# Nested self-attention on one core: loop bodies of two to four tiles written as lists with named PSUM banks, V tiles scaled on ScalarE, and pairs that fall from 512 to 448 and from 160 to 128 rows

## The chip, the cores and the metric

The kernel runs on one core of a Trainium2 chip. The metric is the device time of one execution in microseconds; lower is better. Engines are named as in the profile: PE (matrix engine; PEld is its weight load), DVE (VectorE), ACT (ScalarE), POOL (GpSimd) and SP (SyncE, which here only issues DMAs).

## The reference

```
batch, max_seq, n_heads, head_dim = (32, 512, 8, 64)
lengths = np.random.randint(64, max_seq, size=batch)        # the same draw each time
x: [32, 512, 512] float32, w_qkv: [512, 1536] float32
for b in range(batch):
    x_b = x[b, :lengths[b]]
    q, k, v = split(x_b @ w_qkv)              # 8 heads of 64
    attn = softmax(q @ k.T / 8)               # per head
    output[b, :lengths[b]] = attn @ v         # the other rows are zero
```

## The kernel before

The kernel sorts the 32 sequences by length, longest first, and takes them in pairs. A pair has a class: the row count, out of 512, 480, ... 96 and 340, that holds its longer sequence. For each class there is a loop body, built ahead of time, and all engines branch from body to body by a table of the classes. A body has two **halves**. A half does the attention of one sequence (N rows) and, between its steps, the projections (Q, K, V) of the next one (W rows), so that PE has matmuls while ACT takes exponentials. T is the number of 128-row tiles of N. With the lengths drawn here the halves run in this order (N to W):

| pair | lengths | halves before |
|---|---|---|
| 1 | 502, 447 | 512 to 512, 512 to 480 |
| 2 | 446, 436 | 448 to 448, 448 to 416 |
| 3 | 363, 357 | 384 to 384, 384 to 352 |
| 4, 5 | 351, 347; 343, 333 | 352 to 352 twice; 352 to 340, 340 to 340 |
| 6, 7 | 323, 315; 310, 261 | 340 to 320, 320 to 320; 320 to 288, 288 to 288 |
| 8 | 260, 257 | 288 to 288, 288 to 256 |
| 9, 10 | 246, 230; 223, 220 | 256 to 256, 256 to 224; 224 to 224 twice |
| 11, 12 | 216, 183; 164, 152 | 224 to 192, 192 to 192; 192 to 160, 160 to 160 |
| 13, 14 | 143, 140; 134, 119 | 160 to 160 twice; 160 to 160, 160 to 128 |
| 15, 16 | 101, 86; 79, 75 | one tile: 128 to 96, 96 to 96; 96 to 96, the last |

A pair *drops* when its second sequence is one class lower: the body `drops[N]` then lays the second half at the lower row count. Before the change this is so only inside one tile count and up to 384 rows. Three-tile halves up to 340 rows are *dense*: the scores of one head pair over all key tiles fill both score banks without gaps and are exponentiated in two instructions.

The order of the work in a half is a list of tokens. `S` is a group of score matmuls and its exponential, `D` the dense form; `Q`, `K`, `B` (both) project one head pair for the next sequence; `E` and its end `F`/`G`/`H`/`I` project Q and K in two passes of 64 contraction rows each, in two banks at once; `U`/`W` does the same for two V tiles; `V` is one V tile; `A`/`Z` is the product of probabilities and V for a head pair, with `R` the reciprocal of the row sums and `X` the scaling into `onat`; `O` issues half of the output store from ACT; `c` reads the next class. Scores and `E`/`U` matmuls have 64 contraction rows (64*128 in the profile) and run two at a time; the other projections and `A` have 128. A last V tile of at most 64 rows is done by `vsides` as two column halves side by side (128*64).

PSUM has two score slots of two banks (`s0`, `s1`, tile psc) and four single banks (`a0`, `a1`, tile pa; `v0`, `v1`, tile pav). PE takes a bank with `acquire` (it waits for the engine that emptied it last) and `evacuate` hands it on: Q and K are copied by DVE or ACT (L439, L440), V tiles are always scaled by the row mask on DVE (L463, L559, L560). With `turns` (three-tile halves and 416, 448) the four banks go round; otherwise projections alternate between `a0` and `a1` and `A` takes `v0` and `v1` together.

SP works through its own list for each half: wait until PE has read `xT[h]` (semaphore `s_xtf`), issue the DMA transposes of the next sequence into it (L1603; PE waits for them in `start_proj`), wait for POOL's cast and load the sequence after that (L1614, L1618), zero fill (L1535), store the second half of the output (L1527). POOL writes the ones column of V (L1968, L1969), for which PE waits at the last V tile (`s_on`), and casts x (L1962). Where two-tile bodies end, `bridge` makes the scores for the first one-tile half; there SP stages a transpose (L1740) that POOL copies (L2012).

## Time and profile before

| | us |
|---|---|
| timed runs | 331.85, 333.05, 334.75 (median 333.05) |
| profiled execution: span of the profile | 330.1 |
| PE busy | 316.4 |
| ACT busy | 242.4 |
| DVE busy | 203.6 |
| POOL busy | 68.7 |

The page gives the profiled execution by its span, from the first to the last instruction; a timed run holds, beside such a span, what lies before and after it. Matmuls are pipelined and their ends are modelled, so that successive ones overlap in the profile: how far apart they start says more than how long each shows. In a row, a tile's name stands as output<-inputs, then the shape, then xcount; a stage of the kernel is read by giving a window in us from the span's start.

### The profile page before, as it was taken

How to read it: one execution, taken by the hardware profiler on the slowest of the kernel's cores; microseconds unless marked ns; L12 is line 12 of the kernel's file. 1: busy time of each engine (PE TensorE's matmuls, PEld its weight loads, DVE VectorE, ACT ScalarE, POOL GpSimd, SP SyncE). 2: the span in 40 equal slices, each digit the busy share in tenths (PEclk: the TensorE clock that was granted, in tenths of full speed). 3: DMA queues.
4: the chain of work that ended last, by engine and by line, in shares of the span. 5: the costliest groups of instructions: out<-in, count | busy, mean ns of one | idle time of the engine just before them, and what ended most of it. 6: DMA issues, size and time to landing. Idle time of an engine off the chain costs nothing. (4 is left out here: it accounts for less than half of the span.)

```text
span 330.1 us, 12320 instructions
## 1 busy us (share of the span) xinstructions
PE 316.4 (96%) x4353; PEld 205.5 (62%) x4354; DVE 203.6 (62%) x587; ACT 242.4 (73%) x358; POOL 68.7 (21%) x135
## 2 busy tenths in 40 slices
PE   7899999999999999999999999999999999999880
PEld 2565445455565656656666677677777777677750
DVE  3576576656585575576476557655755566767662
ACT  4577878788889879878778887787677676566531
POOL 3452220201111201210220222022111131131331
PEclk9999999999999999999999999999999999999996
DMA  6957599987656996985997999897689979965952
GB/s 195 341 138 263 94 375 310 292 179 279 153 194 142 326 263 145 323 286 149 283 314 169 235 319 216 214 291 235 212 139 174 214 199 183 170 201 148 200 145 70
DMA packets 83289, 72.42 MB, mean 219 GB/s; under 512 B 41660, under 2 KB 64188, under 8 KB 83204
## 3 DMA queue, kind: packets, MB, share of 16 engines
q1 hardware_dynamic: 69700, 58.27, 70.0%
q10 hardware_dynamic: 13504, 13.11, 11.8%
q8 instruction: 42, 0.69, 0.8%
q14 instruction: 43, 0.35, 0.4%
HBM read 25.32 MB, written 36.70 MB: 188 GB/s over the span
## 5 line engine op out<-in xcount | busy, mean ns | idle before, releaser
L367 ACT ACTIVATE ep<-psc 128x896 f16<-128x896 f32 (+9 forms) x184 | 146.8, 847 | 44.0 <-PE psc L324 34.0
L324 PE MATMUL pa<-xT,w_r 128*128 128x160 f16 (+19 forms) x952 | 127.8, 277 | 1.2 <-PEq L62 1.2
L324 PEld LDWEIGHTS pa<-xT,w_r 128*128 128x128 f16 (+1 forms) x952 | 73.0, 97 | 29.2 <-issue 10.1
L324 PE MATMUL psc<-qkT 64*128 64x224 f16 (+17 forms) x700 | 66.7, 285 | 0.6 <-ACT ep L408 0.4
L324 PE MATMUL pa<-w_r,xT 128*128 128x512 f16 (+4 forms) x332 | 58.6, 328 | 0.3 <-DVE v_aug L560 0.3
L324 PE MATMUL pav<-xT,w_r 64*128 64x352 f16 (+12 forms) x384 | 58.3, 306 | 0.0
L440 DVE CAST qkT<-pa 128x512 f16<-128x512 f32 (+9 forms) x59 | 33.4, 566 | 40.0 <-PE pa L324 36.2
L408 ACT ACTIVATE ep<-psc 128x864 f16<-128x864 f32 (+3 forms) x56 | 49.7, 946 | 10.9 <-PE psc L324 6.5
L324 PE MATMUL pav<-v_aug,ep 128*128 128x65 f16 x1268 | 54.9, 194 | 1.7 <-PEq L62 1.7
L1968 POOL MEMSET v_aug<- 128x256 f16 x28 | 8.8, 313 | 225.5 <-POOLq L1519 225.5
L324 PEld LDWEIGHTS pav<-v_aug,ep 128*128 128x128 f16 x1268 | 48.8, 98 | 10.0 <-issue 3.0
L439 ACT CAST qkT<-pa 128x320 f16<-128x320 f32 (+8 forms) x74 | 34.2, 466 | 16.6 <-PE pa L324 10.8
L661 DVE SCALAR_TENSOR_TENSOR onat<-pav,masks,rcp 128x128 f32<-128x128 f32 (+1 forms) x120 | 41.4, 384 | 4.1 <-DVE rcp L638 1.6
L1962 POOL CAST x<-x_nat 128x1536 f16<-128x1536 f32 (+3 forms) x33 | 42.0, 1272 | 8.6 <-POOLq L1519 8.3
L324 PEld LDWEIGHTS psc<-qkT 64*128 64x128 f16 x700 | 26.7, 94 | 27.2 <-issue 16.7
L463 DVE TENSOR_TENSOR v_aug<-pa,masks 128x512 f16<-128x512 f32 (+1 forms) x46 | 30.8, 674 | 15.0 <-PE pa L324 14.4
L324 PEld LDWEIGHTS pav<-xT,w_r 64*128 64x128 f16 (+1 forms) x384 | 29.8, 95 | 11.6 <-issue 1.6
L324 PEld LDWEIGHTS pa<-w_r,xT 128*128 128x128 f16 (+2 forms) x332 | 22.9, 99 | 18.3 <-issue 4.9
L324 PE MATMUL pav<-w_r,xT 128*128 128x512 f16 (+3 forms) x132 | 24.0, 333 | 0.0
L638 DVE RECIPROCAL rcp<-pav 128x8 f32<-128x8 f32 (+2 forms) x66 | 12.9, 195 | 17.5 <-PE pav L324 14.7
L324 PEld LDWEIGHTS pa<-v_aug,ep 128*128 128x128 f16 x524 | 19.3, 98 | 6.3 <-issue 2.6
L440 DVE CAST qkT<-pav 128x352 f16<-128x352 f32 (+7 forms) x27 | 14.4, 539 | 14.1 <-PE pav L324 13.4
(99 smaller groups left out, 181.4 us busy)
## 6 DMA issues: line engine op xcount, KB each, us to landing
out_dram<-zt SPq DMA_DIRECT2D x16, 768.0 KB, 5.7
x_nat<-in_x_dram SPq DMA_DIRECT2D x12, 512.0 KB
out_dram<-onat ACTq DMA_DIRECT2D x21, 256.0 KB, 3.8
x_nat<-in_x_dram SPq DMA_DIRECT2D x5, 1024.0 KB
out_dram<-onat ACTq DMA_DIRECT2D x12, 384.0 KB, 4.8
out_dram<-onat SPq DMA_DIRECT2D x12, 384.0 KB, 4.4
x_nat<-in_x_dram SPq DMA_DIRECT2D x17, 256.0 KB, 6.5
x_nat<-in_x_dram SPq DMA_DIRECT2D x4, 768.0 KB
```

The source lines that it names most:

```text
L324: return lambda e: e.matmul(o, lhsT, rhs, start=start, stop=stop)
L367: return e.activation(out=dst[at], in_=src[at], func=AF.Exp, scale=scale)
L408: lambda e, par=par, b=b: e.activation(out=ep[:, i, par, 0:T, 0:N], in_=psc_f[:, par, 0 : T * N].rearrange("p (t n) -> p t n", n=N), func= ...
L439: return lambda e: e.copy(out=dst, in_=src)
L440: return lambda e: e.tensor_copy(out=dst, in_=src)
L463: return lambda e: e.tensor_tensor(out=v_aug[h][:, t, lo // HD : lo // HD + n, 0:HD], in0=area[b][:, 0:w].rearrange("p (a d) -> p a d", d=HD),
L638: pr.add("dve", lambda e: e.reciprocal(out=rv, in_=den).then_inc(s_r, 1))
L661: ins = e.scalar_tensor_tensor(scalar=now[0][:, 1, t : t + 1], op0=ALU.mult, op1=ALU.mult, **ops)
L1962: e.tensor_copy(out=x16[h][:, 0:T, :], in_=x_nat[h][:, 0:T, :]).then_inc(s_xc[h], 1)
L1968: e.memset(v_aug[h][:, T - 1, NPAIR:NH, 0:HD], 0.0)
```

## The change

1. All half orders for two, three and four tiles are new lists in which each token names its banks and its evacuating engines: `E3ad:..` means Q by ACT, K by DVE. `e`/`E` are the two passes over Q and K, now in two-tile halves too (`two_cross`); one letter (`E1d`) empties both banks in one instruction. `A10` and `A11` are the parts of one head pair (two query tiles each with four tiles; all three with three tiles, `A10` alone); in two-tile halves `A20` takes head pairs 2 and 3 of query tile 0, and each half makes its own scores `S0` rather than those of the next sequence. `s0` and `s1` can hold a projection (`B1d:s1`).
2. `v_out` and `vsides` can scale on ACT (`V1a`): a Copy with the mask column as scale, read from a [128, 1] operand through a register.
3. Pairs of classes 512 and 480 whose second sequence fits 448 rows drop to 448, pairs of class 160 whose second sequence fits 128 rows drop to 128. Pair 1 becomes 512 to 448, 448 to 448. Pair 14 becomes 160 to 128 and then a one-tile half (`half_one`), with `fall` making its scores; the second output tile is filled with zeros and stored.
4. Second halves of `leave` follow the first halves of `stay` with different banks held (`follow`, `drain`); branch hints and alignment follow the new paths.

The lists that run with these lengths, and the core of the rest:

```diff
-        4: "S S Q0 +A0 S S K0 V0 S S Q1 +A1 S S K1 V1 S S Q2 +A2 S S K2 V2 S S Q3 +A3 S S V3 K3 O",
-        3: "k3 S S E0 E2~ S F0 S I2 S A0 A1 S U0 S S W0 E1~ S S G1 A2 Q3 O A3 S S V2",
-        2: "S S B0 b1 A0 A1 b2 S S V1 b3 A2 O A3 R3 X3 V0",
-    DENSE = "K2 q2 D E1 E3 I1 H3 D k0 c A0 Q0~ A1 D V2 O V1 A2 D A3~ V0"
-    DENSE_OUT = DENSE.replace("D A3~ V0", "V0 D A3")
-    FOUR = "S E1 S G1 S E2 S G2 S E0 S E3 S G0 G3 S S A0 Z0 V1 +A1 S S Z1 V3 +A2 S O S V0 +Z2 S A3 Z3 S S V2"
-    FOUR_SIDES = FOUR.replace("G1", "F1").replace("Z1 V3 +A2", "V3 Z1 A2")
+    LISTS = {
...
+        (512, 448): "S e2:a0,a1 S E2dd S e0:v1,v0 S E0da S e1:a0,a1 S e3:v0,v1 S E1dd S E3dd S A01:a0 A00:a1 c R00 R01 X00 X01 S A10:v0 A11:v1 S S R11 R10 X11 X10 V0d:a0 A20:v1 A21:a1 S S R21 R20 O X21 V1a:a0 X20 V2d:a1 S S V3d:v0 A30:a1 A31:v1 R30 X30 R31 X31",
...
+        448: "S e1:a0,v0 S E1dd S e3:v1,a1 S E3ad S e0:v0,a0 S e2:a1,v1 S c E0da E2dd S S V1d:v0 A00:a1 A01:a0 A10:v1 S R01 R00 X01 S X00 R10 A11:v0 R11 A20:a0 X10 V3a:a1 R20 X11 S S X20 V0d:v1 A21:a1 S A30:v0 O R21 A31:v1 X21 R30 R31 S S X30 X31 V2d:a1",
+        (448, 416): "S e3:a1,v0 S e0:a0,v1 S E3dd S E0dd S S e1:a1,v0 S e2:a0,v1 S E1da E2dd S S V3a:v0 A00:a0 A01:a1 R00 R01 X00 S X01 S c A11:v1 A10:v0 R10 R11 X10 X11 V1a:a0 S S A20:a1 A21:a0 O R20 R21 X20 X21 V0d:v1 S S A30:a1 R30 A31:a0 X30 R31 V2a:v1 X31",
...
+        384: "S e1:a1,v0 S E1d S e0:v1,a0 c S E0ad S A10:v0 A00:a1 R00 S X00 u0:a0,v1 S R10 X10 W0da S S A20:a1 K2a:v0 R20 X20 K3d:a0 S O A30:a1 R30 X30 Q3a:a0 S S Q2d:v0 V2d:a0",
+        (384, 352): "S S e0:v0,v1 e1:a1,a0 S E0ad E1da S S A00:v0 A10:v1 R00 X00 R10 S X10 u0:a1,a0 S S W0da e3:v0,v1 S S E3dd O A20:a1 R20 c X20 Q2a:a0 A30:v0 S S R30 X30 V2d:v1 K2a:a1",
+        352: "S S e0:v0,a0 e1:a1,v1 S E0ad E1da S S A10:a0 R10 A00:v0 X10 R00 S u0:a1,v1 S S X00 W0da e2:v0,a0 S S c E2da Q3a:v1 A20:a1 S S R20 A30:a0 X20 O R30 V2a:v1 X30 K3a:a1",
+        (352, 340): "S S e0:v0,a0 e3:a1,v1 S E0da E3dd S S A10:v0 A00:a1 R10 X10 S R00 u0:v1,a0 S S X00 c W0da e1:a1,v0 S S E1da A20:a0 A30:v1 R20 X20 O V2a:a1 e2:a0,v0 R30 S S X30 E2ad",
+        340: "K2d:a1 V0d:v1 D e0:v0,a1 e1:a0,v1 E0ad E1dd D Q3a:v0 A00:a0 A10:v1 Q2a:a1 R00 X00 R10 c D V1a:v0 X10 V2d:a0 K3a:v1 A20:a1 O R20 A30:a0 D X20 R30 X30",
+        (340, 320): "Q2a:v1 Q3d:v0 V1d:a1 D e0:v1,v0 V2a:a1 Q1d:a0 E0da D A00:a0 K3a:v1 R00 A10:a1 K1a:v0 X00 D R10 A20:v1 X10 R20 O K2a:v0 c X20 V0d:a1 D A30:v1 R30 X30",
+        320: "Q1a:v0 V0a:a0 D V2d:v1 K0a:a1 K1a:a0 K3a:v0 D A00:a1 Q0a:v0 R00 Q2d:v1 X00 A10:a0 R10 D A20:v0 c X10 R20 O X20 Q3d:a1 V1d:v1 D A30:a0 R30 X30 K2d:v0",
+        (320, 288): "K2a:a1 K1a:v1 D Q2d:a0 K0d:a1 Q1d:v0 Q3d:v1 D A00:a1 R00 K3d:v0 A10:v1 R10 X00 Q0a:a0 X10 D A20:v0 R20 X20 c V1a:a1 V2d:v1 D A30:v0 R30 O X30 V0a:a1",
+        288: "Q2d:a0 K3a:v1 D e0:v0,a1 e1:a0,v1 E0da c E1da D K2d:v0 Q3a:v1 A10:a0 R10 A00:a1 D X10 R00 V0a:v0 X00 A20:a0 R20 X20 V2d:v1 D O A30:a1 V1a:v0 R30 X30",
+        (288, 256): "Q2d:v1 D K3d:a1 Q0d:a0 V2d:v1 K1d:a1 D A10:v1 Q3a:a0 K0a:a1 R10 X10 A00:v0 D R00 X00 Q1d:a1 V0d:v1 A20:a0 c R20 X20 O V1d:a1 D A30:v0 R30 K2d:v1 X30",
     }
+    TWO = {
+        False: "S1 e1:a1,a0 S0 e3:v0,v1 E1da E3ad S2 S3 A00:a0 A01:v1 R00 B2a:v0 V1a:a1 X00 A20:a0 R01 X01 R20 X20 O A21:v0 R21 X21 B0a:s1 V0d:v1 c",
+        True: "S1 B1d:s1 e0:a1,a0 e3:v0,v1 E0da S0 S3 E3d c V1d:a1 S2 A00:v1 R00 X00 A01:a0 R01 B2a:s0 X01 O A21:v0 A20:a1 R2 V0a:v1 X20 X21",
+        (256, 256): "S1 S0 e1:a0,a1 E1ad e0:v1,v0 S3 E0ad S2 A00:a1 V1a:a0 A01:v0 R0 B2a:s0 A20:v1 c X01 A21:a0 R20 X00 O X20 R21 V0a:v0 X21 B3d:a1",
+        (256, 224): "S1 S0 e2:a0,v1 e0:v0,a1 c E2dd E0ad S3 S2 A01:v1 A00:a1 R00 R01 X00 X01 B1a:a0 V1d:v0 A21:a1 A20:a0 R2 O X21 X20 B3a:s1 V0d:v1",
+        (224, 192): "S1 S0 e1:a0,a1 e0:v0,v1 E1da E0dd S3 V1a:a0 S2 A00:v1 K2d:a1 Q2d:v0 B3a:s0 A01:a0 R00 X00 c R01 X01 O A20:a1 A21:v0 V0a:v1 R2 X20 X21",
+        (192, 192): "S1 B1d:s1 e0:a0,a1 e2:v1,v0 E0dd S0 E2dd S3 V1d:a0 S2 A00:v0 A01:v1 R0 X00 c X01 B3a:s0 A21:a1 A20:a0 O R2 X20 V0a:s1 X21",
+        (192, 160): "S1 B3d:a0 e1:v1,v0 S0 E1ad e0:a0,a1 S2 E0aa S3 A00:v0 V0a:v1 c R00 A01:a0 X00 R01 B2a:s0 A20:v0 A21:a1 X01 R21 O X21 R20 V1a:v1 X20",
+        (160, 128): "S1 V1d:a0 c S0 e1:v0,a1 V0a:a0 Q2d:v1 E1ad S3 S2 A00:v1 R00 K2a:v0 B0a:a0 B3a:s0 A01:a1 X00 A20:v0 R01 A21:v1 X01 O R2 X20 X21",
+    }
+    def two_order(N, W):
+        return TWO.get((N, W), TWO[W > P and half_rows(W)])
...
-    def v_out(b, h, i, T, of):
+    def v_out(b, h, i, T, of, eng="dve"):
...
+        if eng == "act":
+            def scaled(e):
+                rv = e.snap(regs_act["rank"], min_val=0, max_val=B - 1)
+                return e.activation(
+                    out=v_aug[h][:, t, lo // HD : lo // HD + n, 0:HD],
+                    in_=room[b][:, 0:w].rearrange("p (a d) -> p a d", d=HD), func=AF.Copy,
+                    scale=masks[:, bass.ds(rv, 1), 0, t : t + 1].rearrange("p o t -> p (o t)"),
+                )
...
+    def fall(pr, st, M):
+        for b in list(st["holds"]):
+            acquire(pr, b)
+        acquire(pr, "s0")
+        pr.signals.append(s_xtf[1])
+        scores(pr, 0, 1, 0, 0, 1, M)
...
+            if h and T == 2 and M <= P:
+                half_one(pr, h, W, True)
+            else:
+                half(pr, h, T, (N, M)[h], (M, W)[h], st, last and h == 1)
+            if not h and T == 2 and M <= P:
+                fall(pr, st, M)
...
-    drops = {N: make_body(N, lower[N], lower[N], turn=turn(N)) for N in CLASSES
-             if lower[N] < N and -(-lower[N] // P) == -(-N // P) and N <= 3 * P}
+    drops_at = {N: M for N, M in lower.items()
+                if M < N <= 3 * P and (-(-M // P) == -(-N // P) or M == P)}
+    drops_at.update({N: FOUR_ROWS for N in CLASSES if N > FOUR_ROWS})
+    drops = {N: make_body(N, M, M) for N, M in drops_at.items()}
```

## The prediction

> **What bounds the kernel now.** I read the page first, its head and its DMA line, then the busy time by stage (cut where the matrix engine's queue takes up a new sequence's transposed input), then the timeline of a short stretch, then two views of waits.

> ```profile
> span 330.1 us, 12320 instructions
> ...
> PE 316.4 (96%) x4353; PEld 205.5 (62%) x4354; DVE 203.6 (62%) x587; ACT 242.4 (73%) x358; POOL 68.7 (21%) x135
> ...
> DMA  6957599987656996985997999897689979965952
> ```

> PE is busy for 96% of the span. Its ends are modelled, though, so that share alone doesn't say how much a better order could win. By stage:

> ```profile
> core 0: us, PE busy (x) PEld busy (x) DVE busy (x) ACT busy (x) POOL busy (x), PEclk, DMA share, GB/s
> ...
> 24.65:62.08 37.43, 37.43 (x413) 18.80 (x414) 24.09 (x57) 29.99 (x32) 6.60 (x7) 1.00 0.92 253
> 62.08:97.13 35.05, 35.03 (x492) 20.25 (x490) 22.54 (x69) 29.40 (x38) 4.58 (x6) 1.00 0.78 232
> 97.13:157.36 60.23, 60.19 (x859) 36.51 (x856) 37.29 (x112) 50.38 (x80) 9.45 (x15) 1.00 0.79 228
> 157.36:235.61 78.25, 77.64 (x1176) 54.50 (x1173) 49.42 (x164) 61.58 (x93) 13.08 (x21) 1.00 0.93 245
> 235.61:263.36 27.75, 27.75 (x351) 20.85 (x348) 15.40 (x41) 20.55 (x28) 6.19 (x12) 1.00 0.92 193
> 263.36:311.85 48.49, 47.38 (x743) 35.90 (x741) 33.45 (x91) 31.25 (x57) 11.67 (x24) 1.00 0.84 180
> ```

> These are the 512 pair, the 448 pair, the loose three-tile halves, the dense ones, 256 and 224, and the 192 and 160 rows down to the one-tile tail. PE has work throughout at the full clock, ScalarE 64% to 84%, VectorE less. So PE ends each stage; but the DMA engines are at 0.92 and 0.93 in three of them, which matters below. What a matmul costs, and what PE loses between matmuls:

> ```profile
> 299.82 0.38 PE L324 MATMUL pa<-w_r,xT 128*128 128x512 f16 x1
> ...
> 300.13 0.45 PE L324 MATMUL psc<-qkT 64*128 64x160 f16 x8
> ...
> 300.51 1.41 PE L324 MATMUL pa<-xT,w_r 128*128 128x160 f16 x16
> ...
> 303.28 0.63 PE L324 MATMUL pa<-w_r,xT 128*64 128x256 f16 x8
> ...
> 304.99 1.04 PE L324 MATMUL pa<-w_r,xT 128*128 128x512 f16 x4
> ...
> 308.76 0.61 PE L324 MATMUL pa<-w_r,xT 128*128 128x256 f16 x4
> ```

> One 512-column matmul shows 0.38 and four show 1.04, so in a stream they start 0.22 apart. Four of 512 columns and four of 256 differ by 0.43 over 1024 columns: 0.42 ns a column. The 64-row scores run two at a time (eight of 160 columns in 0.45). Now the joints: the 512-column matmul of 299.82 lets the next start at 300.04, but the scores start at 300.13. Their four pairs take 4 x 0.07, to 300.41, but the 128-row projection starts at 300.51. So **each switch between 64-row and 128-row matmuls costs 0.09 to 0.10**, and so, I take it, does one into or out of the two-column form (128*64) of a short last V tile. What else PE's weight loads wait for inside the halves (window 24 to 311):

> ```profile
> PEld psc L324 <- ACT ep L367: 2.3, 8, 0.4
> PEld pa L324 <- DVE qkT L440: 1.6, 5, 0.4
> PEld pav L324 <- DVE qkT L440: 1.3, 4, 0.4
> ...
> PEld psc L324 <- ACT ep L408: 0.5, 1, 0.5
> PEld pa L324 <- DVE v_aug L463: 0.4, 2, 0.2
> PEld pa L324 <- DVE v_aug L560: 0.4, 1, 0.4
> ```

> 6.5 us together, in 28 halves: all that any order of evacuations can give back, and part of it lies behind a running matmul.

> **The change part by part.** The sum is made against the execution of 330.1 us span; the three timed runs are 331.85 to 334.75, so 1.8 to 4.7 lie around such a span. I take the difference off the median, 333.05.

> *512 falls to 448.* Of the drawn lengths only the first pair (502, 447) does. Its first half projects a 448-row partner: 32 Q/K matmuls and 4 pairs of scores, 64 columns fewer each, 36 x 64 x 0.42 ns = 0.97; and the last V tile goes in the two-column form, 0.63 instead of 1.04: 0.41. Its second half has 12 pairs of scores with 64 columns fewer, 32 projections with 32 fewer (the next class is laid at 448, not 480) and 4 pairs with 32 fewer: 1920 x 0.42 ns = 0.81, and the V tile again 0.41. Together **-2.6**, all on PE.

> *The order of the four-tile halves.* Counting the places where a list goes from 64 to 128 rows or back (two-column V counted, and the step to the next half): 16 and 16 in the old order of 512, 11 and 11 with the new lists; 448: 11 and 11 before, 11 and 9 after. 12 x 0.095 = **-1.1**.

> *The other lists, counted in the same way.* Loose three-tile 30 before, 31 after; dense 47 and 55; the halves of 256 and 224 lose 9 (scores now stand beside the crossed projections, which also have 64 rows); 192 and 160 gain 5. In all +5: **+0.5**. These lists spend switches to shorten waits; of the 6.5 us above I give them 1.4, a fifth, since half of the waits stand where data supply sets the pace (next): **-1.4**. The ends are 0 (new waits where the old were) and 6.5.

> *What is late next: the transposed input.* A half can start its projections only when SP has issued the DMA transposes and they have landed.

> ```profile
> 48.50 8.37 SPq L1603 DMA_TRANSPOSE xT<-x  x4
> ...
> 57.42 0.83 SPq L1614 DMA_DIRECT2D x_nat<-in_x_dram  x1
> ```
> ```profile
> xT<-x SPq DMA_TRANSPOSE x80, 3.8
> ```
> ```profile
> 62.84 0.36 PE L324 MATMUL psc<-qkT 64*128 64x448 f16 x2
> ```

> The four transposes for the third half (448) are issued from 48.50 to 56.87, behind loads, fills and a store, the last from about 55.6; with the median 3.8 to landing that is 59.4. The half begins at 62.84 now. After 3.6 of gain (2.6 in columns, ten switches) it would begin at 59.2 and want them one score group later, 0.2. By these medians it waits little; a landing 1 us later than the median costs 1 us. SP's own queue in the two stretches where PE is loaded most lightly:

> ```profile
> SPq L1519 <- SPq L1519: 0.3, 1, 0.3
> ```
> ```profile
> SPq L1519 <- SPq L1519: 3.3, 4, 2.0
> ```

> The first is 192 to 228 (dense), the second 264 to 312 (192 and 160). In 36 us SP waits 0.3: it works without a pause and PE cannot outrun it there by more than the lead it has. In 264 to 312 it waits 3.3, of which 2.0 at once. I take **+0.5** for waits on input (0 to 2).

> *160 falls to 128 and the tail.* One half loses 32 x 32 columns of Q/K (0.43) and the two-column V tile (0.4); the next becomes a one-tile half: 32 projections of 128 columns (1.8), one V tile (0.9) and an estimated 0.5 for scores and output, 3.2 where the rows below have 4.9 (305.95 to the last scores at 310.9), so 1.7 less. But:

> ```profile
> 305.95 0.45 PE L324 MATMUL psc<-qkT 64*128 64x160 f16 x8
> ...
> 306.45 0.31 POOL L1968 MEMSET v_aug<- 128x256 f16 x1 [4.39 <-POOLq L1519]
> ...
> 306.70 0.25 POOL L1969 CAST v_aug<-masks 128x16 f16 x1
> ...
> 306.84 1.22 SPq L1603 DMA_TRANSPOSE xT<-x  x1
> ...
> 310.67 0.40 PE L324 MATMUL psc<-qkT 64*128 64x128 f16 x8
> ...
> 311.93 1.40 PEld L324 LDWEIGHTS pa<-xT,w_r 128*128 128x128 f16 x32 [1.03 <-issue]
> ```

> The half before the tail starts at 305.95, its transpose for the next is issued at 306.84, and PE stands 1.03 before the projection at 311.93: about 5 us from issue, whatever PE does meanwhile. A shorter half only lengthens that stand. The new list of the falling half also puts a V piece second, which waits for POOL's ones: here POOL ends 1.0 after its half starts, the scores ahead of the piece take 0.3, so PE stands some 0.7 there with everything of that half queued behind it. I cost the fall at **0** (a gain of 2.5 less the 0.7, so 1.8, if the transposes land early enough; a loss of 0.7 if nothing is given back).

> *V tiles scaled on ScalarE.* 36 V pieces of the executed lists move.

> ```profile
> L463 DVE TENSOR_TENSOR v_aug<-pa,masks 128x512 f16<-128x512 f32 x43 | 29.6, 691 | 14.8 <-PE pa L324 14.2 <-DVEq L62 0.3
> ```
> ```profile
> L439 ACT CAST qkT<-pa 128x512 f16<-128x512 f32 x3 | 1.8, 585 | 0.9 <-PE pa L324 0.8
> ```

> No row shows a scaled copy on ScalarE; the plain one of that size takes 585 ns, VectorE's scaling 691. At 585 the move adds 21 us to ScalarE over the 287 us of the table in which it idles 64: hidden, if no exponential that PE needs soon stands behind one. I cost it at 0 (to 21 x 1/3, the rival below). [...]

> Sum: -2.6 - 1.1 + 0.5 - 1.4 + 0.5 + 0 + 0 = -4.1; 333.05 - 4.1 = **328.9**.

> **Rivals.**
> *The waits go.* The lists win most of the 6.5 and input holds nothing: -2.6 - 1.1 + 0.5 - 5 = -8.2, 324.9. For it: the 6.5 are spread thinly, 0.2 to 0.5 each, so a short reordering can remove each. Against it: SP's 0.3 us of pause in the dense stretch.
> *Supply takes it.* The third half, the dense stretch and the 160 rows wait for transposes, and the eight extra dense switches stay: -3.7 + 0.5 + 0.8 + 1.5 = -0.9, 332.1. For it: DMA shares of 0.92 and 0.93. Against: SP still has pauses elsewhere (3.3 after 264).
> *Slower: ScalarE becomes the bound.* A V piece ahead of an exponential holds the score bank 585 ns longer and PE with it. It decides where a half has no ScalarE time left; the four-tile stage is nearest, 29.40 of 35.05. If one in three of the 36 pieces holds PE for its length that is 7.0: -3.7 + 0.5 + 7.0 = +3.8, 336.9. Against it: even the tightest stage leaves ScalarE over 5 us in 35.

> **How the numbers follow.** Forecast 0.48 (327.3 to 330.6), waits go 0.22 (324 to 327.3), supply takes it 0.22 (330.6 to 334), slower 0.08 (336.5 up). The range for 8 in 10, 324.9 to 333.2, takes in the forecast and three quarters of the first two rivals. A measurement of this kernel tells about 1% from no change: below 329.7 lie three quarters of the forecast and all of the first rival, 0.57; within 1% 0.35; above 336.4 0.08.

> **What would show it.** Right: the first two halves shorter by 1.9 and 1.7; PE's weight loads for the scores wait fewer times by "issue" in the first 97 us; the halves of 256 and 224 shorter by 0.2 each; ScalarE about 20 us busier, VectorE as much less; in the tail a longer stand before the projection after the fall, near 1.0 + 1.7 + the little gained. Wrong: PE idle behind exponentials in the four-tile stage, or a third half that starts over 1 us after its list allows, or SP pausing in the dense stretch while PE still gains.

## The result: 3.3% to 3.7% slower, and the profile after

The changed kernel took **346.39 us** (median; 343.94 to 350.05) beside 333.16 for the kernel before: a ratio of 1.0374, 95% interval 1.0311 to 1.0436. The same kernel, run once more beside the experiments, took 344.16 (343.44 to 344.74; 1.0328, 1.0282 to 1.0374). Forecast were 328.9, at most 333.2: the sign was wrong. The profile shown here is that of the second set; a median takes in all runs of its set, while a ratio and its interval leave out the slow ones, over 1.5% above the fastest of their kernel (among them the first set's profiled execution, 350.05, and four of the ten runs of `h3` below, whose other six have a median of 331.3).

The head of the page of the changed kernel:

```profile
span 342.1 us, 12769 instructions
...
PE 318.0 (93%) x4497; PEld 204.2 (60%) x4498; DVE 191.8 (56%) x609; ACT 256.4 (75%) x386; POOL 68.6 (20%) x136
```

PE has 12 us more span and is busy for a smaller share of it: it isn't given more work, it stands. Busy time by stage of the changed kernel, cut at the same places as the table of before:

```profile
core 0: us, PE busy (x) PEld busy (x) DVE busy (x) ACT busy (x) POOL busy (x), PEclk, DMA share, GB/s
24.59:64.10 39.51, 36.25 (x490) 20.51 (x490) 22.30 (x71) 31.21 (x38) 6.61 (x7) 1.00 0.92 267
64.10:104.00 39.90, 35.71 (x487) 19.99 (x488) 19.75 (x62) 31.40 (x41) 4.59 (x6) 0.96 0.65 177
104.00:166.70 62.70, 62.48 (x863) 36.59 (x861) 33.97 (x108) 54.55 (x88) 9.32 (x15) 1.00 0.81 232
166.70:245.60 78.90, 77.47 (x1114) 52.87 (x1112) 46.90 (x156) 65.13 (x96) 13.04 (x21) 1.00 0.91 235
245.60:275.70 30.10, 29.13 (x422) 21.59 (x423) 16.39 (x57) 22.66 (x35) 5.95 (x13) 1.00 0.79 182
275.70:325.40 49.70, 45.88 (x800) 33.95 (x800) 31.27 (x102) 32.99 (x61) 11.70 (x24) 1.00 0.71 170
```

Against before: four-tile stage +6.9 (79.4 for 72.5), loose three-tile +2.5, dense +0.7, 256 and 224 +2.4, 192 to the tail +1.2. Where PE was busy 37.43 of 37.43 and 35.03 of 35.05, it is now busy 36.25 of 39.51 and 35.71 of 39.90, and the second row has a granted clock of 0.96.

To part work from waiting I took, from the traces, how far successive matmuls start apart: what their columns take at 0.42 ns is work (two that run side by side counted once), the rest is loss. Up to the last matmul (323.1 before, 336.2 after) **work fell by 4.4, from 278.3 to 273.9, and losses rose by 17.5, from 44.7 to 62.2**; after it the end came 1.1 sooner. The weight loads' waits of the changed kernel, window 24 to 325, those for another engine:

```profile
PEld psc L348 <- ACT ep L391: 9.4, 22, 3.1
PEld pa L348 <- DVE qkT L464: 5.5, 13, 2.0
...
PEld pa L348 <- ACT qkT L463: 1.7, 5, 0.5
PEld pa L348 <- DVE v_aug L497: 1.4, 3, 0.9
```

The rows of this kind (with six small ones of 0.3 to 0.9) sum to 21.2, where before they summed to 6.5. The two longest, 3.1 and 2.0, aren't a matter of the order of a list. The timeline where the first body is left for the second (class 448):

```profile
63.98 0.69 DVE L497 TENSOR_TENSOR v_aug<-pa,masks 128x512 f16<-128x512 f32 x1 [0.50 <-DVEq L66]
...
65.33 0.93 PE L348 MATMUL pa<-xT,w_r 64*128 64x448 f16 x8
67.96 1.73 ACT L391 ACTIVATE ep<-psc 128x896 f16<-128x896 f32 x2 [3.14 <-issue]
68.13 1.16 DVE L464 CAST qkT<-pa 128x448 f16<-128x448 f32 x2 [3.46 <-issue]
68.93 0.10 PEld L348 LDWEIGHTS psc<-qkT 64*128 64x128 f16 x2 [3.11 <-ACT ep L391]
68.93 0.55 PE L348 MATMUL psc<-qkT 64*128 64x448 f16 x2 [2.67 <-ACT ep L391]
```

PE waits for an exponential (that much the prediction had named as a sign of its failure). But ScalarE isn't late because it is busy: its own idle time, and VectorE's, is "issue", time in which the engine waits for nothing that the profile shows. In the trace the last instruction that both engines take up before it is the branch into the next body (63.3 and 64.1), then come 4.4 and 3.9 us of nothing (the rows' 3.14 and 3.46 count from the end of the work before). In that time packets of the queues that the page calls "instruction" move, one of 16 KB from 64.0 and three of 8 KB from 65.7 to 66.4, while the DMA share is over 1. What follows it, by stretches:

```profile
64.10:65.90 1.80, 1.80 (x18) 0.85 (x20) 0.58 (x1) 0.72 (x1) 1.01 (x3) 1.00 1.05 368
65.90:68.90 3.00, 0.36 (x4) 0.00 (x0) 0.77 (x2) 0.94 (x2) 1.28 (x1) 1.00 1.12 180
68.90:72.30 3.40, 3.37 (x20) 1.36 (x22) 0.39 (x1) 2.50 (x3) 0.00 (x0) 0.50 0.77 101
```

PE stands for 2.8 (2.67 in the row, which counts from the modelled end), and then runs **3.4 us at half the granted clock**: nine steps that cost 180 ns more each, 1.6. The jump costs 4.4 in all. The first jump (into the body of the fall) shows VectorE alone standing:

```profile
29.11 0.38 PE L348 MATMUL psc<-qkT 64*128 64x512 f16 x2
...
29.74 1.69 DVE L464 CAST qkT<-pa 128x448 f16<-128x448 f32 x3 [3.91 <-issue]
...
31.04 0.36 PE L348 MATMUL pa<-xT,w_r 64*128 64x448 f16 x2 [1.55 <-DVE qkT L464]
```

Another 1.7. That the engines stand here because their instructions have not come yet is my reading of these rows and of the packets above; no row names what they wait for, and as many packets move at the second joint of the kernel before (64.9 to 67.5), where nothing is lost.

**Theory**: the lists do what was counted, but three things that the sum didn't have take more: (A) behind the jumps into and out of the new body VectorE, ScalarE or PE stand, by where the code lies; (B) the class read `c` now stands where it stops PE's queue; (C) the new lists have tighter seams. **Rivals**: ScalarE is overloaded by the V pieces; the falls themselves cost; the new lists are simply worse.

### The profile page after: what moved, and what is told of

The parts are those of the page before. It is cut to its first block, busy times and chain, and to the rows that moved or that the text cites. A ratio compares the mean times of both kernels' runs of the same rounds, so it can differ in the third digit from the quotient of the medians.

```text
span 348.4 us, 12769 instructions
## 1 busy us (share of the span) xinstructions
PE 320.0 (92%) x4497; PEld 206.4 (59%) x4498; DVE 191.9 (55%) x609; ACT 257.2 (74%) x386; POOL 68.4 (20%) x136
## 5 line engine op out<-in xcount | busy, mean ns | idle before, releaser
L391 ACT ACTIVATE ep<-psc 128x896 f16<-128x896 f32 (+8 forms) x182 | 144.1, 841 | 30.5 <-PE psc L348 19.1
L348 PE MATMUL pa<-xT,w_r 64*128 64x448 f16 (+19 forms) x1392 | 134.3, 289 | 7.0 <-PEq L66 3.3
L348 PEld LDWEIGHTS pa<-xT,w_r 64*128 64x128 f16 (+1 forms) x1392 | 77.9, 97 | 45.6 <-issue 13.4
L464 DVE CAST qkT<-pa 128x448 f16<-128x448 f32 (+12 forms) x107 | 51.6, 502 | 71.3 <-PE pa L348 58.2
L348 PE MATMUL psc<-qkT 64*128 64x448 f16 (+16 forms) x692 | 70.1, 287 | 4.6 <-ACT ep L391 3.0
L348 PEld LDWEIGHTS pa<-v_aug,ep 128*128 128x128 f16 x1768 | 61.2, 98 | 17.3 <-issue 9.7
L348 PE MATMUL pa<-v_aug,ep 128*128 128x65 f16 x1768 | 68.9, 195 | 2.2 <-PEq L66 1.4
L348 PEld LDWEIGHTS psc<-qkT 64*128 64x128 f16 x692 | 28.3, 95 | 34.7 <-issue 18.1
L635 DVE SCALAR_TENSOR_TENSOR onat<-pa,masks,rcp 128x128 f32<-128x128 f32 x136 | 40.8, 343 | 2.2 <-DVE rcp L618 0.5
L463 ACT CAST qkT<-pa 128x352 f16<-128x352 f32 (+9 forms) x77 | 32.3, 432 | 12.2 <-PE pa L348 7.2
L490 ACT ACTIVATE v_aug<-pa,masks 128x512 f16<-128x512 f32 (+1 forms) x29 | 19.9, 687 | 13.1 <-ACTq L66 6.6
```

The source lines that it names most:

```text
L348: return lambda e: e.matmul(o, lhsT, rhs, start=start, stop=stop)
L391: return e.activation(out=dst[at], in_=src[at], func=AF.Exp, scale=scale)
L463: return lambda e: e.copy(out=dst, in_=src)
L464: return lambda e: e.tensor_copy(out=dst, in_=src)
L490: return e.activation(out=v_aug[h][:, t, lo // HD : lo // HD + n, 0:HD], in_=room[b][:, 0:w].rearrange("p (a d) -> p a d", d=HD), func=AF. ...
L635: ins = e.scalar_tensor_tensor(scalar=now[0][:, 1, t : t + 1], op0=ALU.mult, op1=ALU.mult, **ops)
```

## The experiments

Times are medians of interleaved runs, with the ratio to the kernel before and its 95% interval; "last matmul" is from the profiled execution, since the end behind it scatters by 2 us.

**The two falls and the V pieces.** The kernel unchanged (344.16 above):

> The changed kernel as it stands, run again for a profile at the full clock: 343 to 345 us. If the 6 us that the four-tile stage (to about 103 us) lost in the first profile were only its lower clock, that stage now ends within 1.5 us of the kernel before; if the lists lose them, it still ends 4 to 6 us later.

Without the fall from 160 to 128:

```diff
-                if M < N <= 3 * P and (-(-M // P) == -(-N // P) or M == P)}
+                if M < N <= 3 * P and -(-M // P) == -(-N // P)}
```

> Pairs of 160 no longer fall to 128 (160 to 160, then 160 to 128, as before); all else as changed. Theory 'the fall asks for late input': its second token needs the transposed input, PE stands 5.0 us there and 2.0 more in the tail, so about 7 us come back: 336 to 338. Rival 'the fall is free, the loss sits in the lists': 343.5 to 346 (my sum gave the fall a gain of 1.8 to a loss of 0.7).

350.04, 1.0487 (1.0426 to 1.0548): **5.9 slower**, not faster, which neither side had expected. The bridged half took 9.63 us in its place of 5.14: PE stood 2.1 at 325.8, while VectorE was still emptying banks, and then again ran at half clock (0.50 from 327.8 to 334.6). With these lists the fall pays.

Without the fall from 512 to 448:

```diff
-    drops_at.update({N: FOUR_ROWS for N in CLASSES if N > FOUR_ROWS})
```

> Pairs of 512 no longer fall to 448 (512 to 512, then 512 to 480, in their new lists). My sum priced the columns at 2.6 us, so 345.5 to 347.5. Rival 'the list written for 512 to 448, with six projections in front of its first attention, loses more than the columns win': 341 to 343.

343.2, 1.0263 (1.0184 to 1.0343): 1.0 less than with the fall, which its runs (339.15 to 343.75) don't separate. The last matmul of the profile starts at 333.0 against 336.2. The four-tile stage ends at 98.6, against 104.0 with the fall and 97.1 before: 5.3 of the stage's 6.9 of loss go with the body of the fall, though 2.6 us of columns come back.

All V pieces on VectorE:

```diff
-        384: "... W0da ... V2d:a0",
+        384: "... W0dd ... V2d:a0",      (and each V1a:a0 as V1d:a0, in all lists)
```

> All V tiles scaled on VectorE again, in the same places of the lists. Theory 'ScalarE's pieces hold the exponentials': 7 us come back, 336 to 339. Rival (my sum) 'they are hidden': 343 to 346, with ScalarE about 20 us less busy and VectorE about 20 more.

354.55, 1.0656 (1.0593 to 1.0719). The page's head:

```profile
PE 316.4 (90%) x4497; PEld 204.4 (58%) x4498; DVE 213.6 (61%) x651; ACT 234.9 (67%) x344; POOL 68.7 (19%) x136
```

ScalarE is relieved by 21.5, and the kernel loses **10.4**. The rival "ScalarE is the bound" is refuted. The 10.4 aren't the price of the pieces alone, for this edit moves code too: a branch of PE took 2.5 at 307.6, with PE standing 1.9 behind it, while the stall at the exit was 0.7 shorter and had no half clock behind it. In the changed kernel a piece takes on ScalarE

```profile
L490 ACT ACTIVATE v_aug<-pa,masks 128x512 f16<-128x512 f32 (+1 forms) x29 | 19.9, 688 | 14.0 <-ACTq L66 7.6 <-PE pa L348 5.4 <-issue 0.8
```

0.69, as on VectorE (691 ns before). That two engines empty banks side by side is what counts is my reading; no run separates it.

**The class read.** PE's rows in the second half; between scores and projection, which start 0.19 apart in `g1_cmove` below, PE waits for nothing of another engine:

```profile
50.56 0.37 PE L348 MATMUL psc<-qkT 64*128 64x448 f16 x2
51.51 0.74 PE L348 MATMUL pa<-xT,w_r 64*128 64x448 f16 x6 [0.58 <-PEq L66]
```
```profile
L1443 PEldq TENSOR_LOAD <-codes x15: 298/310/1034, 50.6 to 330.4; - x15
```

The read lasts 0.30 to 1.03 on PE's own queue. Before, it lasted as long (0.30 to 1.03), and the gaps behind it came to 0.6 in all. In the new lists it often stands among 64-row pairs, and they come to 3.8. Moved in eight lists, for example

```diff
-        448: "... e2:a1,v1 S c E0da E2dd S S V1d:v0 A00:a1 ..."
+        448: "... e2:a1,v1 S E0da E2dd S S V1d:v0 c A00:a1 ..."
```

> Only the token c (the read of the next class) is moved, in eight lists, to stand right behind a projection or V tile of 128 rows. Theory 'PE stands while its queue reads the class': the gaps around these reads, 3.8 us in the changed kernel against 0.6 before, fall under 1: 340.5 to 342. Rival 'the read only covers another wait that then shows': 343.5 to 345.

341.0, 1.0203 (1.0132 to 1.0274), as expected; last matmul 333.2, **-2.9**. The gap at 50.6 is gone:

```profile
49.95 0.37 PE L348 MATMUL psc<-qkT 64*128 64x448 f16 x2
50.14 1.69 PE L348 MATMUL pa<-xT,w_r 64*128 64x448 f16 x16
```

**Bringing the code nearer: attempts that missed.** `f1_near` was to lay the body of the fall beside its callers. In the built program the blocks of the engines kept their order; only the alignment at the entry moved. So it, and the runs below with the same edit, tell of the alignment alone.

```diff
-                if not fetch and k == 0:
+                if not fetch and k == 2:
                     e.addr_align(FETCH // 2, offset=LEAD[name], max_nops=0)
```

> Only the place of code changes, for VectorE and ScalarE: the body that falls from 512 to 448 is laid right behind the opening, and the class 448 right behind it, so that neither engine jumps far there. Theory 'instruction supply': after the two branches VectorE stood 2.8 and 3.9 us and ScalarE 4.4 us before the next instruction; these fall under 0.7 us, the PE stalls of 1.7 and 2.8 us go, and with them the 3.3 us at half clock that follow the second (1.6 us lost): 338 to 340. Rival 'the two engines wait for data, wherever their code lies': 343.5 to 345.

346.27, 1.0403 (1.0356 to 1.045): VectorE's gap at the entry went (first half 17.59 for 19.88), and its gap at the exit grew from 3.9 to 4.9. The first holds in every profile here: in the nine of kernels with the body of the fall that keep this alignment VectorE stands 1.2 to 2.8 behind the branch into it, in the nine without it 0.14 at most. With the class read moved too:

> Both edits at once. If the two losses stand in different places and add up: 335 to 337.5. If the waits of the lists take up what is freed: 338 to 341.

342.75, 1.0234 (1.015 to 1.0317); the exit gap was 6.7. And with no alignment at all:

> As the run with both edits, but the alignment ahead of class 448 is left out for VectorE and ScalarE, so that nothing lies between the end of the falling body and that class. Theory 'supply, and the padding pushed the target out of what is already there': VectorE's gap of 4.9 to 6.7 us at the end of the 512 pair falls under 0.7 us, the PE stall (3.4) and the half clock behind it (1.6) go: 335 to 337.5. Rival 'the stall at this place has another cause than the place of the code': 340 to 343.

341.03, 1.0258 (1.0168 to 1.0348), exit gap 6.3. One edit that moves addresses cures one jump and worsens the next.

**The old order within the changed kernel**, written in the new tokens, for example four tiles (first half):

```diff
-        (512, 448): "S e2:a0,a1 S E2dd S e0:v1,v0 S E0da ..."
+        (512, 448): the old FOUR, with the banks that the old turn gave
```

> The order, banks and engines of before for all halves of three and four tiles, written as lists of the new form; both falls, the two-tile lists and the far jumps stay. Theory 'the new lists of these halves lose some 5 us in class reads and in banks that are emptied late': 338 to 340.5. Rival 'these lists are even or better, as my sum had it (minus 2.0)': 344 to 347.

348.16, 1.0467 (1.0415 to 1.0519). This conversion gave both halves the same banks, where the old turn goes on in the second half, so that dense halves lost 7.6: it says nothing on the lists. Done faithfully, for three and four tiles, with the class read moved in the two-tile lists and no alignment:

> The order, banks and engines of before in three- and four-tile halves, now with the turn of the banks that each half of a pair had (the earlier run gave both halves the first one's, which cost the dense halves 7 us); both falls kept, the near layout, the moved class reads in two-tile halves. Theory 'the lists lose, the falls win': before's 333 less 2.7 of columns, plus some 1.5 for the two-tile lists and less 0.5 in the tail: 330 to 333. Rival 'the new frame costs by itself (joined copies, row maxima of waits)': 335 to 338.

337.87, 1.0193 (1.0118 to 1.0268), where the rival was expected; last matmul 327.8. Stage by stage it equals the kernel before within 0.2, except the first two halves (-1.7), two tiles (+2.4), and the third half, 22.76 for 18.24. That is VectorE's exit gap, 5.8, and not the frame that the rival blames. With four tiles alone in the old order:

> The same with the old order in four-tile halves alone; three-tile halves keep the new lists with moved class reads. Against the run with all old lists it prices the new three-tile lists: by the traces 1.3 (loose) and 1.7 (dense) of loss, less 1.1 for the moved reads, so 1 to 3 us slower than that run. Rival 'the new three-tile lists are no worse': within 0.7 of it.

342.6, 1.0287 (1.0226 to 1.0348): 4.7 slower than that run, above the 1 to 3 expected; but here PE also stood 2.3 at 228.4 for transposed input, with half clock behind it, so it doesn't price the lists. The exit gap (6.4) stays whichever lists run; it belongs to where the code lies.

**What lies between.** Class 480 isn't used by these lengths, but its bodies lay between the fall and class 448: the jump passed 277 VectorE instructions, counted in the built program, where the longest in the kernel before passes 155. (Distance isn't all: the jump at the entry passes only 88, and there the alignment decides, 1.2 to 2.8 us with it and at most 0.14 without.) `h1` leaves the class out (59 are passed), moves the class reads and drops the alignment:

```diff
-CLASSES = sorted([STEP * k for k in range(3, 17)] + [DENSE_ROWS], reverse=True)
+CLASSES = sorted([STEP * k for k in range(3, 17) if k != 15] + [DENSE_ROWS], reverse=True)
```

> The changed kernel with the moved class reads, without the class 480 (no pair here begins in it) and without the alignment for VectorE and ScalarE: the jump out of the falling 512 pair is 58 instructions of VectorE instead of 275. Theory 'the target of a long jump must be fetched first': VectorE's gap there falls from 4 to 6 us to under 0.7, and 5 us come back against the run with moved reads alone: 335 to 337. Rival 'it stands there for another reason': 339.5 to 342.5.

**334.85, 1.0072 (1.0029 to 1.0114)**; last matmul 325.2: eleven of the thirteen us lost up to there are back, with all new lists in place. VectorE has no idle time over 0.5 us put down to "issue". The first four stages of `h1`:

```profile
23.90:61.30 37.40, 35.83 (x490) 20.30 (x488) 22.97 (x71) 32.18 (x39) 6.60 (x7) 1.00 0.90 236
61.30:96.20 34.90, 33.73 (x485) 19.62 (x486) 19.19 (x61) 30.32 (x40) 4.58 (x6) 1.00 0.88 253
96.20:158.50 62.30, 62.10 (x863) 36.69 (x861) 33.86 (x108) 54.36 (x88) 9.30 (x15) 1.00 0.84 232
158.50:236.10 77.60, 76.95 (x1112) 52.78 (x1112) 46.98 (x156) 65.14 (x96) 13.02 (x21) 1.00 0.92 239
```

With the old order for three and four tiles as well:

> The same with the old order of three- and four-tile halves. The run with the long jump had its last matmul at 327.9; 4.5 less: 323.4 (before: 323.05), so 331.5 to 334. If the jump stays: 336 to 339.

334.55, 1.0101 (0.9998 to 1.0203); last matmul 322.7. In these two profiles the new lists of three and four tiles cost 2.5 to there: 2.0 in the four-tile stage, 2.2 in the loose one, while the dense one gains 1.1. The medians differ by only 0.3. With the old order for two tiles too (only the falls are left):

> The same, and two-tile halves in the old order too; what is left of the change are the two falls. If each fall gives what its columns say (2.7 and about 2, part of the second lost to the later transposes): 328.5 to 331, and the two-tile lists cost 2.5 to 4 against the run before it. If the falls give nothing in the old order either: 332 to 334.

334.11, 0.9996 (0.9941 to 1.0052); the stage of 256 and 224 falls from 29.6 to 27.8, but a stand of PE of 1.7 at 61.0 and a slower tail put its last matmul at 324.8. That stand is for the third half's transposed input:

```profile
47.70 11.66 SPq L1873 DMA_TRANSPOSE xT<-x  x4
```
```profile
62.69 0.93 PE L348 MATMUL pa<-xT,w_r 64*128 64x448 f16 x8 [1.72 <-PEq L66]
```

The last of the four was issued at 56.3 and landed at 62.4. `h1` stands 0.9 at the same place, `h2` not at all.

Class 480 alone left out of the changed kernel:

> The changed kernel with one edit: no class of 480 rows, which none of these sequences needs (the pair of 502 and 447 falls to 448 either way). Its code no longer lies between the body of the fall and the 448 body, so that the jump out of the fall passes far fewer instructions; the class reads and the alignment at the entry stay. Theory (what instructions a long jump has to fetch): the gaps of VectorE and ScalarE of some 4 us on entering 448 go, and with them PE's stall of 2.8 and the 1.6 at half clock: about 4.4 less, 339 to 340.5; the entry gap of 2.7 on VectorE stays. Rival (the gap belongs to the new lists' first exponential and projection, whatever lies between): 343 to 345, the gap still there.

342.39, 1.0274 (1.0198 to 1.0351). The third half is

```profile
63.00:80.70 17.70, 17.51 (x245) 9.94 (x244) 10.05 (x31) 15.52 (x21) 2.30 (x3) 1.00 0.72 201
```

17.64 by PE's own marks, where it was 21.99: **-4.35, with the full clock**; the gaps of both engines there are gone and the one at the entry has stayed (3.83), as the theory had it. The total missed what was expected by 2. ScalarE's 1.8 of nothing behind its branch at 230.0 is no such jump: it waits for scores, and PE stands 1.0 there for a transpose that lands at 230.6. Such stands of PE come to 3.4 in this execution, where the changed kernel's come to 1.1.

**The fall alone.** The kernel before, without class 480 and with 512 falling to 448, without and with its alignment:

```diff
-             if ... and -(-lower[N] // P) == -(-N // P) and N <= 3 * P}
+             if ... and -(-lower[N] // P) == -(-N // P) and (N <= 3 * P or N > FOUR_ROWS)}
```

> The kernel before, with the fall from 512 to 448 alone (without the class 480, so that the jump is short). My first term alone: 333 less 2.6, 329.5 to 331. Rival 'the columns saved are only waited for elsewhere (the third half's transposes)': 332 to 333.5.

> The kernel before without class 480 and with 512 falling to 448, and here with the alignment of the entry that the kernel before had (the earlier run of this without it had ScalarE stand 7.2 us behind the branch at 23.0). Theory (ScalarE's stand is an instruction fetch that hangs on where the code lies): the stand of 7.2 goes back to about 1.2 and the fall gives its columns, 2.6: 329.5 to 332. Rival (the fall itself costs its columns again, by joints between its halves): 335 to 338 with the stand gone.

337.95, 1.0172 (1.0068 to 1.0276), and 337.18, 1.0119 (1.0048 to 1.0189): slower than either side expected. ScalarE stands behind its branch at 23.0, but it waits for scores, and PE for its own branch:

```profile
L1346 PEldq COMPARE_BRANCH  x17: 63/339/6504, 23.2 to 315.1; - x17
```
```profile
24.60:29.60 5.00, 0.00 (x0) 0.00 (x0) 0.67 (x3) 0.00 (x0) 0.00 (x0) 0.68 1.01 376
29.60:33.00 3.40, 3.11 (x26) 1.62 (x27) 0.00 (x0) 1.94 (x2) 3.34 (x4) 0.50 0.21 76
```

A branch that takes PE 0.34 in the median takes 6.5 here (6.4 in the first of the two), with a DMA share of 1.01, and the granted clock is 0.50 from 26.4 to 33.2. Alignment had no part in it: that expectation missed. From PE's first mark behind it to the last matmul the two take 299.2 and 297.8, the kernel before 298.4: the 2.6 of columns don't show as time here.

> The changed kernel with all old orders, so only the two falls, without class 480, and with the alignment at the entry kept (the earlier run of this without it came out equal to the kernel before). Theory (where the entry's code lies sets how long the first body starves): up to 2 less than without, 331 to 333; rival (the alignment plays no part in it): 333.5 to 335.

334.88, 1.0064 (1.0029 to 1.0099) with the alignment, 334.11 and 0.9996 without: no gain, where the rival was expected. One line of alignment changes VectorE's first conversion in the body of the fall from

```profile
27.67 1.16 DVE L464 CAST qkT<-pa 128x448 f16<-128x448 f32 x2 [1.29 <-PE pa L348]
```

(without) to

```profile
29.44 1.69 DVE L464 CAST qkT<-pa 128x448 f16<-128x448 f32 x3 [3.74 <-issue]
```

and the half, part of it at half clock, from 17.60 to 21.52; other halves gave most of it back. No version beat the kernel before by a measurable amount.

## Why the prediction was wrong, point by point

- **Columns, -2.6: right as work, in part as time.** Work in the four-tile stage fell from 64.2 to 61.3. Where VectorE doesn't stand at the entry, the first half gives 1.6 to 1.7 (`h1` 17.72, `h2` and `h3` 17.60, before 19.34), close to the 1.9 foreseen. The second half, foreseen 1.7 shorter, is nowhere shorter (19.7, 18.4 and 19.9 in these runs, before 18.1).
- **Switches, -1.1 and +0.5: right.** Their price held (97 and 98 ns in the median), the two-column form included. Counted as the prediction counts them, they went from 193 to 185 behind the opening, eight fewer where seven were forecast (53 to 41 in the four-tile stage, 49 to 57 in the dense one).
- **Waits given back, -1.4: the step that failed in sign.** The rows grew from 6.5 to 21.2. It treated the waits as something that an order can only lower and bounded it by 0 below, from a row of the old order. The lists' own seams (a bank whose V piece or exponential is emptied late, 0.25 to 0.8 each) cost 2.5 in three and four tiles (`h1` against `h2`; 0.9 of it is the wait for input that `h2` hasn't), and 1.8 in 256 and 224 (`h2` against `h3`), each by one profile. The halves of 256 and 224, foreseen 0.2 shorter each, are 0.6 longer.
- **Terms that were missing: the step that failed in size.** The sum put the jumps and the class read at nothing, without a reason. Jumps: 1.7 at the entry, 2.8 + 1.6 at the exit, 6.1 in all (taking them away gave 2.3 in `f1_near`'s first half and 4.35 in `n480`). The class read: 3.2 by its gaps, 2.9 by `g1_cmove`. The diff showed both (a new body, `c` at other places, alignment), and the trace of before had their rows: branch, then the first instruction; the read's 0.3 to 1.0 on PE's queue. I took neither for an operation with a price. With seams of 3.4 that makes 12.7 of the 17.5, an estimate, since each is read in another layout; the other 5 are spread over halves that differ from run to run and aren't assigned.
- **Transposed input, +0.5 (0 to 2): it came, and was too small.** In the changed kernel's second profile the jumps kept PE behind its input (stands of PE that end with a landing of `xT` sum to 1.1, before to 0.9), and SP, which paused 0.3 in the dense stretch, pauses 3.6. Where VectorE no longer stood at the entry, PE stood in some runs where the prediction had said, at the third half: 0.9 in `h1`, 1.5 in `fg2`, 1.7 in `h3`, whose transposes took 6.1 from issue to landing instead of 3.8; in all `h3` has 4.7 of it. So `h3` waits for much of what its columns win, as "Supply takes it" had it. In the first set's profiled execution it is 6.6, most of it at the fall from 160 to 128, for a transpose that landed at 318.5:

```profile
310.64 2.67 SPq L1819 DMA_TRANSPOSE xT<-x  x1
```
```profile
318.81 1.01 PE L348 MATMUL pa<-w_r,xT 128*128 128x256 f16 x4 [4.82 <-PEq L66]
```

- **160 to 128, at 0:** in the second profile the stand for POOL's ones came (0.8; 0.7 foreseen), and the longer stand in the tail did not (1.1 for 0.9 before):

```profile
314.84 0.31 POOL L2186 MEMSET v_aug<- 128x256 f16 x1 [4.92 <-POOLq L1735]
...
315.10 0.26 POOL L2187 CAST v_aug<-masks 128x16 f16 x1
...
315.50 0.60 PE L348 MATMUL pa<-w_r,xT 128*128 128x256 f16 x4 [0.84 <-PEq L66]
```

 Its own worth was shown only against the new lists without it, 5.9 by another body's stall; both falls together on the old lists (`h3`) come out at 0.9996.
- **V on ScalarE, at 0:** the cover held: ScalarE 14 busier, VectorE 12 less (20 foreseen). A piece takes 688 ns in the mean, not the 585 of the sum. That it was worth nothing by itself failed: without it the new lists lose 10, part of it by moved code.
- **Rivals.** "ScalarE becomes the bound" had the sign, and the wrong engine: PE stood 2.8 behind an exponential that was late behind a branch, with ScalarE doing nothing for 4.4. "Supply takes it" shows in part once the jumps are cured. None of the four cases held the jumps and the class read, and 0.08 for slower was far too little for a change that replaces every list and every body.

## What to carry to other kernels

When a change adds or moves bodies that are branched to, look in the trace for what each engine does behind every branch, and give the new jumps a term: here one cost 1.7 to 6.5 us of PE. Where the code lies decided it here: at the exit what lies between, even a class that never runs (VectorE stood 3.2 to 7.2 us with it, at most 0.5 without), at the entry a line of alignment (1.2 to 2.8 with it, at most 0.14 without). Look also for what covers a register read from memory on the queue of the engine that sets the pace: reads of 0.30 to 1.03 us left gaps of 0.6 in all before and of 3.8 in the new lists. A stand can be paid once more: behind the 2.8 at the exit came 3.4 us at half clock, 1.6 lost. And what such a stall hides, here input that comes late (stands of 0.9 to 1.7 at the third half), shows when the stall is cured.
